# A hybrid attention and RWKV-7 layer on one core: every engine's queue in the order of the text

## The chip, the cores and the metric

The kernel runs on one NeuronCore of a Trainium2 chip. Its engines are TensorE (PE, and PEld for its weight loads), VectorE (DVE), ScalarE (ACT), GpSimd (POOL) and SyncE (SP, which here only issues transfers). Each engine works through its own queue in order; an instruction that waits for a semaphore holds all that stand behind it in that queue. The metric is the device time of one execution in microseconds, lower is better.

## The reference

One layer, float32, 256 context tokens and 1,024 latent tokens. One input projection feeds two branches whose outputs share one output projection:

```python
q, k, v, g_a, u_b, g_b = jnp.split(h @ lp['w_in'], ...)
# branch A, 8 heads, blocks of 128 queries, latents see 512 cached + 1024 own keys
s = jnp.einsum('bqhmd,bkhmd->bhmqk', qblk, k).astype(F32) * scale
p = jax.nn.softmax(s, axis=-1)
a = p[:, :, 0] - lam * p[:, :, 1]
o = jnp.einsum('bhqk,bkhv->bqhv', a, v)          # then an RMS norm over 128 values
# branch B, 16 heads of 64, both directions, one step per token
sa = jnp.einsum('bhvk,bhk->bhv', S, -kk_t)
S = S * w_t[:, :, None, :] + sa[..., None] * b_t[:, :, None, :] + v_t[..., None] * k_t[:, :, None, :]
y = jnp.einsum('bhvk,bhk->bhv', S, r_t)
# y of both directions is added, normalized per head, gated
x = x + gate[:, None, :] * (jnp.concatenate([o_a, o_b], axis=-1) @ lp['w_out'])
```

At the end comes one RMS norm per token row.

## The kernel before

**First stage.** The input projection runs 128 columns at a time over all tokens, with the preparation of both branches beside it; it spills operands to DRAM. The change leaves it as it was.

**Recurrence stage** (`mix_phase`). The scan is done in chunks of 32 tokens. An item is four pairs of heads and one segment of 256 tokens in both directions; there are 10 items of 8 chunks, so 80 calls of `step`. A step's chain is: 32 small matmuls into `bank[0]` (L895, the corrections), copies of these into the operand tile `R` (L903, the first pair of duos by ScalarE, the second by VectorE, four copies each), matmuls into `bank[1]` (L915, the new state), VectorE multiplies by the decay into the next `R` (L926), matmuls of the outputs (L938) and a ScalarE copy of them to `ys` (L940). Both sets of copies read the same PSUM bank, and the framework lets only one engine read a bank at a time, so the second engine's copies wait for the first's. Operands of two steps (a part) lie in one of two slots, and `load_part` fetches the next part into the other.

Between the pieces of the chain, `fill` puts other work, at a fixed rate per step: items of the attention (the generator `attention`), `norm` (the scan's outputs), `output`, `project` (the output projection, 10 tiles for each of four sets of columns), and the inverses that GpSimd makes for later items. Attention takes a block of 128 queries through `scores` (matmuls into `sc`, of which there are two buffers; VectorE negates, bounds by the running minimum and writes them to `pb`, L1061; after the last chunk ScalarE takes the exponential, L1069), `weight` and `combine` (VectorE: map 1 times its factor added to map 0, L1082), `trans` (TensorE transposes, a ScalarE copy to `aT`) and `values` (matmuls into `po`).

**After the recurrence** the generators run out: the last attention blocks, the last tiles of `project`, and `final`. It takes the rows of 128 tokens one after another: load `of`, `x` and the sum so far `y`; split into `ohi` (ScalarE) and `olo` (GpSimd); 24 matmuls into both banks; VectorE adds; GpSimd multiplies by the gate; VectorE adds to `x`; square, root and scaling; store. Eight of the ten rows do all this at once; the first two do their last part at the very end.

**What sets the order.** TensorE's queue has the order of the text from this stage on; the other engines' queues are sorted by the framework's scheduler, which plays the program through with estimated durations, by

```python
ctx.enter_context(tc.manual_schedule(engines={nc.tensor.engine}))
```

and `with ahead(HPC)` lets it take the recurrence's copies and multiplies earlier. In an order by hand that has no effect.

Of the kernel before, what the change touches and what calls it, by code (L numbers as in the profile page):

```python
# [10 lines left out]
F32 = mybir.dt.float32  # L11
# [37 lines left out]
TBUF = 1  # L49
YBUF = 1  # L50
NDEL = 10
# [691 lines left out]
def mix_phase(ctx, tc, i, o, s, ident, nhalf, dram, td0, neglam, subg, lnh, heads, psm):  # L743
# [137 lines left out]
    def ahead(n):  # L881
        return tc.high_priority(offset=n) if n else nullcontext()

    def step(j, k, fill):
        m, f = j // NF, j % NF
        c = HN * f + k
        p0, sg = items[m]
        hv = lambda h: slice(64 * h, 64 * h + 64)
        for w in duos:
            L, R = slots[w, j % 2]  # L890
            for d in range(2):
                for e in range(2):
                    for h in range(2):
                        u = 64 * e + 32 * h
                        nc.tensor.matmul(bank[0][u:u + 32, P * w + 64 * d:P * w + 64 * d + 64], L[0:96, e, h, d, k, 96:128],  # L895
                                         R[0:96, k, d, e, hv(h)], start=True, stop=True, tile_position=(0, u))
        with ahead(HPC):
            for w in duos:
                R = slots[w, j % 2][1]
                for e in range(2):  # L900
                    for h in range(2):
                        u = 64 * e + 32 * h
# [14 lines left out]
        with ahead(HPC):  # L917
            for w in duos:
# [9 lines left out]
        g = c // 4  # L928
        if c % 4 == 0:
            ysb[m, g] = cp.tile([P, 4, NL, HD], F32, tag="ys", name=f"ys{m}_{g}", bufs=YBUF)  # L930
# [9 lines left out]
        nc.scalar.copy(ysb[m, g][:, c % 4], bank[0][:, 256:512].rearrange("p (x v) -> p x v", x=NL))  # L940
        if later_prep:
# [3 lines left out]
    def store_y(m, g):  # L945
        p0, sg = items[m]
        y = ysb.pop((m, g))
        for d in range(2):
            t0 = tok0(sg, d)
            for h in range(2):  # L950
                q = 64 * d + 32 * h
                dst = s["y"][p0 // NL, t0:t0 + SEG, d, h].rearrange("(c t) w v -> t c (w v)", t=CH)
                dst = (dst[:, ::-1] if d else dst)[:, 4 * g:4 * g + 4]
                nc.sync.dma_start(dst, y[q:q + 32].rearrange("t c x v -> t c (x v)"))
# [6 lines left out]
    def norm(p, g0):  # L961
# [14 lines left out]
        nc.sync.dma_start(bv, s["bv"][rows, cols].rearrange("(x p) t -> p x t", p=P))  # L976
        yield
        yield
        m = pool.tile([P, 2, 4], F32, tag="m", name=f"m{nm}", bufs=2)
        r = pool.tile([P, 8], F32, tag="r", name=f"r{nm}", bufs=2)  # L980
        nc.gpsimd.tensor_tensor(y[0], y[0], y[1], op=ALU.add)
        yield
        yield
        nc.vector.tensor_reduce(m, v4(y[0]), op=ALU.add, axis=AX.X)
        nc.vector.tensor_scalar(m, m, 1.0 / HD, None, op0=ALU.mult)
        for t in range(2):
            mean = m[:, t].rearrange("p (h x) -> p h x", x=2).unsqueeze(3).broadcast_to([P, 2, 2, HD])
            nc.gpsimd.tensor_tensor(y[1][:, t].rearrange("p (x h v) -> p h x v", x=2, v=HD), y[0][:, t].rearrange("p (h x v) -> p h x v", x=2, v=HD), mean,
                                    op=ALU.subtract)
# [54 lines left out]
    def attention():  # L1044
        blocks = [(h, qb) for h in range(heads) for qb in (FORD if h == heads - 1 else range(NT))]
        st = {}

        def scores(n, m, c):
# [14 lines left out]
            if c < nk - 1:  # L1063
                return
            w = kn * nk
            ns = 1 if nk == 1 else ES
            for k in range(ns):
                v = pm[:, w // ns * k:w // ns * (k + 1)]
                nc.scalar.activation(v, v, AF.Exp, bias=mn[:, c:c + 1], scale=-1.0, accum_out=B["l"][:, m, B["b"]:B["b"] + 1])  # L1069

        def weight(n):
            h, qb = blocks[n]
            B = st[n]
            l, b = B["l"], B["b"]
            nc.vector.reciprocal(B["cc"], l[:, 1, b:b + 1])
            nc.vector.scalar_tensor_tensor(B["cc"], B["cc"], l[:, 0, b:b + 1], neglam, op0=ALU.mult, op1=ALU.mult)
# [96 lines left out]
        for n in range(NB + 2):  # L1173
# [23 lines left out]
            cost = 0.45 if nk == 3 else 0.25  # L1197
            vp = []
            if pp is not None:
                vp = [(pp, c) for c in range(1 if len(st[pp]["ch"]) > 1 else 0, len(st[pp]["ch"]))]  # L1200

            def old_values():
                if vp:
                    values(*vp.pop(0))

            for c in range(nk):
                scores(n, 0, c)
                yield cost
                if c < nk - 1 and vp:
                    old_values()  # L1210
                    yield 0.87
            while vp:
                old_values()
                yield 0.87
            for c in range(max(nk, kp_)):
                if c < kp_:
                    trans(p, c)
                    yield 0.43
                if c < nk:
                    scores(n, 1, c)  # L1220
                    yield cost
            if new:
                weight(n)
                for c in range(nk):
                    combine(n, c)
            if kp_ > 1:
                values(p, 0)
                yield 0.87
            if new and h + 1 < heads:
# [12 lines left out]

    def load_wo(nm, sl, whi, wlo, ks, g=None):
        for k in ks:
            for n in range(2):
                c = slice(n * 512, n * 512 + 512)
                w = op.tile([P, 512], F32, tag="wst", name=f"wst{nm}_{k}_{n}", bufs=2)
                nc.sync.dma_start(w, i["w_out"][0, sl[k]:sl[k] + P, c])
                if g is not None:
                    nc.gpsimd.tensor_tensor(w, w, g[:, c], op=ALU.mult)  # L1250
                nc.scalar.copy(whi[:, k, c], w)
                nc.gpsimd.tensor_tensor(wlo[:, k, c], w, whi[:, k, c], op=ALU.subtract)
                if n:
                    yield

# [132 lines left out]

    ctx.enter_context(tc.manual_schedule(engines={nc.tensor.engine}))
    att = attention()  # L1390
# [13 lines left out]
    def at(t, f):  # L1404
        later.setdefault(t, []).append(f)
# [24 lines left out]
    for t in range(n_tick):  # L1430
# [14 lines left out]
        step(j, k, fill)  # L1445
        if c % 4 == 3:
            at(t + 1, lambda m=m, g=c // 4: store_y(m, g))
        if c < NC - 1:
# [106 lines left out]
```

## Time and profile before

| | |
|---|---|
| Median of three runs | 2617.71 us (2614.24 to 2619.5) |
| Profiled execution | 2608.0 us, span 2606.2 us |
| TensorE busy, of the span | 88%, mean granted clock 0.938 |
| VectorE, ScalarE, GpSimd busy | 59%, 46%, 45% |
| Transfers over the span | 437.55 MB, mean 168 GB/s |

A busy share is an average over stages with different limits, and matmuls are pipelined, so that a busy TensorE is not one at its peak. The clock is a share of TensorE's full 2.4 GHz.

### The profile page before, as it was taken

What the parts mean: (1) busy time and instruction counts of PE and PEld (TensorE: products, weight loads), DVE (VectorE), ACT (ScalarE), POOL (GpSimd) and SP (SyncE); (2) the same over time, 40 slices, a digit from 0 to 9 for tenths busy, and PEclk for the clock granted to TensorE, in tenths of its full rate; (3) what the DMA queues carried; (4) which work ended last, traced back from release to release, by engine and by line L of the source; (5) the groups of instructions that cost most, each with busy time, mean ns of one, the idle gap of its engine ahead of it and who ended that gap; (6) DMA issues with size and microseconds to landing.
All of it is one profiled execution on the core that took longest, in us unless ns stands there. A gap on an engine that the chain in (4) does not pass through costs nothing.

```text
span 2606.2 us, 60633 instructions
## 1 busy us (share of the span) xinstructions
PE 2295.6 (88%) x23907; PEld 1895.5 (73%) x23907; DVE 1547.9 (59%) x3210; ACT 1194.9 (46%) x2530; POOL 1172.6 (45%) x1725
## 2 busy tenths in 40 slices
PE   5999999999999999898678888877998898986786
PEld 4888888888888888787466666666776676775675
DVE  5656565546455655533467776766655565665567
ACT  3334443334333343322356665655555554553353
POOL 4234343243433442465374777587722311225264
PEclk9999999999999999998789898888899998998898
DMA  7465656566646564567978797878879779868335
GB/s 240 109 162 134 176 148 179 135 164 168 151 126 168 138 181 114 171 162 173 220 146 176 155 182 140 163 156 191 205 168 220 181 182 218 193 157 242 124 118 179
DMA packets 516732, 437.55 MB, mean 168 GB/s; under 512 B 156551, under 2 KB 460851, under 8 KB 511328
## 3 DMA queue, kind: packets, MB, share of 16 engines
q1 hardware_dynamic: 514352, 427.94, 67.0%
q0 software_dynamic: 2096, 5.75, 1.1%
q8 instruction: 188, 3.08, 0.5%
q14 instruction: 96, 0.79, 0.1%
HBM read 258.69 MB, written 163.86 MB: 162 GB/s over the span
## 4 chain that ended last, share of the span: by engine, by line
PE 47%; DMA 18%; DVE 11%; POOL 9%; SPq 5%; ACT 5%; issue 4%; POOLq 0%; DVEq 0%; ACTq 0%
PE sc L1058 3%; PE pg L451 3%; DVE pb L1082 2%; PE po L1105 2%; DMA wst<-w_out 2%; PE bank L915 2%; DVE pb L1061 2%; PE pso L1299 2%; PE pa L1090 2%; DMA acc<-acc 2%; PE pso L1301 1%; PE ptk L455 1%; PE pso L1300 1%; DMA yn<-y 1%; DVE R L926 1%
## 5 line engine op out<-in xcount | busy, mean ns | idle before, releaser
L1058 PE MATMUL sc<-ka,q 128*128 128x512 f32 (+1 forms) x832 | 315.7, 470 | 73.9 <-DVE pb L1061 64.4
L1069 ACT ACTIVATE pb<-pb,mn 128x1536 f32<-128x1536 f32 (+1 forms) x160 | 218.3, 1365 | 126.6 <-DVE pb L1061 125.4
L1061 DVE TENSOR_SCALAR_CACHE_REDUCE pb<-sc,mn 128x512 f32<-128x512 f32 x256 | 191.8, 749 | 74.6 <-PE sc L1058 64.5
L1105 PEld LDWEIGHTS po<-vk,aT 128*128 128x128 f32 x1600 | 216.2, 200 | 23.9 <-ACT ob L1111 3.3
L1105 PE MATMUL po<-vk,aT 128*128 128x128 f32 x1600 | 225.4, 286 | 4.1 <-ACT ob L1111 2.0
L1058 PEld LDWEIGHTS sc<-ka,q 128*128 128x128 f32 x832 | 143.9, 213 | 110.6 <-DVE pb L1061 84.2
L736 POOL TENSOR_TENSOR tmp<-aw,tt 128x31 f32<-128x31 f32 (+15 forms) x310 | 165.4, 534 | 121.4 <-DMA L<-kt 33.6
L481 POOL TENSOR_SCALAR ta<-ta,ka 128x256 f32<-128x256 f32 x80 | 87.1, 1089 | 291.9 <-DVE bk L479 291.8
L458 ACT COPY km<-ptk 64x256 f32<-64x256 f32 x320 | 117.6, 368 | 183.1 <-PE ptk L455 149.5
L738 POOL TENSOR_TENSOR tt<-tt,tmp 128x31 f32<-128x31 f32 (+15 forms) x310 | 182.4, 589 | 20.5
L1090 PE MATMUL pa<-ident,pb 128*128 128x128 f32 x800 | 139.3, 300 | 45.5 <-DVE pb L1082 19.7
L1082 DVE SCALAR_TENSOR_TENSOR pb<-pb,cc,pb 128x512 f32<-128x512 f32 (+1 forms) x208 | 169.8, 866 | 2.3
L1090 PEld LDWEIGHTS pa<-ident,pb 128*128 128x128 f32 x800 | 105.8, 154 | 79.9 <-issue 21.9
L452 DVE TENSOR_TENSOR km<-pg,msk 128x512 f32<-128x512 f32 x80 | 55.1, 688 | 176.2 <-PE pg L451 155.0
L808 ACT COPY L<-yb 32x384 f32<-32x384 f32 x312 | 146.6, 470 | 27.5 <-PE yb L805 23.1
L903 DVE COPY R<-bank 32x128 f32<-32x128 f32 x320 | 92.6, 289 | 103.3 <-ACT R L903 92.1
L926 DVE TENSOR_TENSOR R<-bank,wc 64x256 f32<-64x256 f32 x312 | 131.0, 420 | 37.8 <-PE bank L915 28.8
L1092 ACT COPY aT<-pa 128x512 f32<-128x512 f32 (+1 forms) x208 | 116.2, 569 | 73.0 <-PE pa L1090 69.1
L1061 DVE TENSOR_SCALAR_CACHE_REDUCE pb<-sc 128x512 f32<-128x512 f32 (+1 forms) x160 | 101.4, 636 | 51.6 <-PE sc L1058 49.4
L1299 PE MATMUL pso<-wohi,ohi 128*128 128x512 f32 x240 | 104.5, 435 | 30.7 <-ACT ohi L1282 17.3
L1283 POOL TENSOR_TENSOR olo<-of,ohi 128x512 fp32r<-128x512 f32 x30 | 39.5, 1315 | 200.5 <-ACT ohi L1282 183.6
L915 PEld LDWEIGHTS bank<-R,L 128*64 128x64 f32 x2560 | 95.9, 145 | 35.5 <-issue 12.2
(355 smaller groups left out, 6432.2 us busy)
## 6 DMA issues: line engine op xcount, KB each, us to landing
kt<-km SPq DMA_DIRECT2D x160, 256.0 KB
L<-kt SPq DMA_DIRECT2D x80, 512.0 KB
acc<-acc SPq DMA_DIRECT2D x50, 512.0 KB
ra<-ra SPq DMA_DIRECT2D x160, 128.0 KB
L<-ra SPq DMA_DIRECT2D x80, 256.0 KB
R<-vb SPq DMA_DIRECT2D x160, 64.0 KB
y<-ys SPq DMA_DIRECT2D x80, 128.0 KB
yn<-y SPq DMA_DIRECT2D x40, 256.0 KB
```

The source lines that it names most:

```text
L736: e.tensor_tensor(mv, aw[:n, t, t + 1:CH].unsqueeze(2).broadcast_to([n, w, j]), tt[:n, t:t + 1, 0:j].broadcast_to([n, w, j]), op=ALU.mult)
L738: e.tensor_tensor(tt[:n, t + 1:CH, 0:j], tt[:n, t + 1:CH, 0:j], mv, op=ALU.add)
L808: nc.scalar.copy(L[96:128, :, q // 2, q % 2, :, 0:96], pp[32 * q:32 * q + 32, 0:192 * HN].rearrange("p (e c y) -> p e c y", e=2, y=96))
L915: nc.tensor.matmul(bank[1][hv(h), o_:o_ + 64], L[:, e, h, d, k, 0:64], R[:, k, d, e, hv(h)], start=True, stop=True, tile_position=(0, 64 * h))
L926: nc.vector.tensor_tensor(dst[:, :, :, hv(h)], bank[1][hv(h), 256 * w:256 * w + 256].rearrange("p (d e v) -> p d e v", e=2, d=2), wcs[p0][ ...
L1058: nc.tensor.matmul(sc, q[:, v, m, qc], ka[:, m, 0:kn], start=(v == 0), stop=(v == 1))
L1061: nc.vector.tensor_scalar(pm[:, c * 512:c * 512 + kn], sc, -0.125, mn[:, c - 1:c] if c else None, op0=ALU.mult, op1=ALU.min, accum_out=mn[ ...
L1069: nc.scalar.activation(v, v, AF.Exp, bias=mn[:, c:c + 1], scale=-1.0, accum_out=B["l"][:, m, B["b"]:B["b"] + 1])
L1082: nc.vector.scalar_tensor_tensor(a, B["p"][1][:, v], B["cc"], a, op0=ALU.mult, op1=ALU.add)
L1090: nc.tensor.transpose(pt[:, t * P:(t + 1) * P], B["p"][0][:, 512 * c + t * P:512 * c + (t + 1) * P], ident)
L1105: nc.tensor.matmul(po, B["aT"][c][:, t * P:(t + 1) * P], vk[:, t, :], start=(c == 0 and t == 0), stop=(c == last and t == nt - 1))
L1299: nc.tensor.matmul(ps, ohi[:, k - k0, :], whi[:, k, c], start=(n == 0), stop=False)
```

## The change

- `manual_schedule` names all five engines: from the recurrence stage to the end of the kernel every queue has the order of the text. The other edits move text to suit.
- Corrections: the columns of `bank[0]` are laid out by duo, so that four copies of 32x256 (two by VectorE, which comes first, two by ScalarE) take the place of eight of 32x128.
- `attention`: an exponential is written behind the item that follows its last scores; `weight` and `combine` of a block stand among the items of the next block, one at a time, and `values` runs wholly two blocks later.
- `store_y` writes each part's outputs (two chunks, 160 transfers of half the size in place of 80), from two buffers instead of one.
- `norm`: four turns between load and use instead of two; the addition of the directions and the subtraction of the mean go from GpSimd to VectorE.
- `load_wo`: a piece of the output weights is split two loads after its own load.

```diff
-YBUF = 1
+YBUF = 2
...
-        with ahead(HPC):
-            for w in duos:
-                R = slots[w, j % 2][1]
-                for e in range(2):
-                    for h in range(2):
-                        u = 64 * e + 32 * h
-                        (nc.vector.tensor_copy if w else nc.scalar.copy)(
-                            R[96:128, k, :, e, hv(h)], bank[0][u:u + 32, P * w:P * w + P].rearrange("p (d v) -> p d v", d=2))
+            R = slots[w, j % 2][1]
+            for h in range(2):
+                u = 64 * w + 32 * h
+                (nc.scalar.copy if w else nc.vector.tensor_copy)(
+                    R[96:128, k, :, :, hv(h)], bank[0][u:u + 32, 0:256].rearrange("p (d e v) -> p d e v", d=2, e=2))
...
-        yield
-        yield
+        for _ in range(4):
+            yield
...
-        nc.gpsimd.tensor_tensor(y[0], y[0], y[1], op=ALU.add)
-        yield
-        yield
+        nc.vector.tensor_tensor(y[0], y[0], y[1], op=ALU.add)
...
-            w = kn * nk
-            ns = 1 if nk == 1 else ES
-            for k in range(ns):
-                v = pm[:, w // ns * k:w // ns * (k + 1)]
-                nc.scalar.activation(v, v, AF.Exp, bias=mn[:, c:c + 1], scale=-1.0, accum_out=B["l"][:, m, B["b"]:B["b"] + 1])
+            v = pm[:, 0:kn * nk]
+            soon.append(lambda: nc.scalar.activation(v, v, AF.Exp, bias=mn[:, c:c + 1], scale=-1.0,
+                                                     accum_out=B["l"][:, m, B["b"]:B["b"] + 1]))
...
+            def item(f, r, *a):
+                f(*a)
+                if late:
+                    late.pop(0)()
+                late.extend(soon)
+                soon.clear()
+                return r
+
+            vq = [(pp, c) for c in range(len(st[pp]["ch"]))] if pp is not None else []
+            for c in range(max(nk, len(vq))):
+                if c < nk:
+                    yield item(scores, cost, n, 0, c)
+                if c == 2 and cb:
+                    combine(p, cb.pop(0))
+                if c < len(vq):
+                    yield item(values, 0.87, *vq[c])
+                if c == 1 and cb:
+                    weight(p)
+                    combine(p, cb.pop(0))
...
             for c in range(max(nk, kp_)):
+                if c < nk:
+                    yield item(scores, cost, n, 1, c)
+                if cb:
+                    combine(p, cb.pop(0))
                 if c < kp_:
...
+                    yield item(trans, 0.43, p, c)
...
-    ctx.enter_context(tc.manual_schedule(engines={nc.tensor.engine}))
+    ctx.enter_context(tc.manual_schedule(engines={e.engine for e in (nc.tensor, nc.vector, nc.scalar, nc.gpsimd, nc.sync)}))
```

VectorE's queue in the recurrence stage, before: the scores of block 1 of a head (`mn_1`; `pb_12288` is its buffer), and between them the factor and the three combinations of block 0 (`cc_0`), which stand in one run, with the copies of the corrections behind them.

```order
L1061 TENSOR_SCALAR pb_12289,mn_0_15864<-sc_0_1_2_15960,mn_0_15864 128x512
L1061 TENSOR_SCALAR pb_12288,mn_1_15970<-sc_1_0_0_15972 128x512
L1061 TENSOR_SCALAR pb_12288,mn_1_15970<-sc_1_0_1_15985,mn_1_15970 128x512
L1075 RECIPROCAL cc_0_15865<-l_0_15862 128x1
L1076 SCALAR_TENSOR_TENSOR cc_0_15865<-cc_0_15865,l_0_15862,neglam 128x1
L1082 SCALAR_TENSOR_TENSOR pb_12287<-pb_12289,cc_0_15865,pb_12287 128x512 x3
L903 COPY R_11584<-bank_12282 32x2x64 x4
L1061 TENSOR_SCALAR pb_12288,mn_1_15970<-sc_1_0_2_16035,mn_1_15970 128x512
```

VectorE's queue at such a place, after: the scores of block 6 (`mn_6`) with the combinations of block 5 (`cc_5`).

```order
L1058 TENSOR_SCALAR pb_12287,mn_6_15196<-sc_6_0_0_15198 128x512
L1058 TENSOR_SCALAR pb_12287,mn_6_15196<-sc_6_0_1_15209,mn_6_15196 128x512
L901 COPY R_11564<-bank_12282 32x4x64 x2
L1070 RECIPROCAL cc_5_15029<-l_4_14790 128x1
L1071 SCALAR_TENSOR_TENSOR cc_5_15029<-cc_5_15029,l_4_14790,neglam 128x1
L1077 SCALAR_TENSOR_TENSOR pb_12288<-pb_12289,cc_5_15029,pb_12288 128x512
L1058 TENSOR_SCALAR pb_12287,mn_6_15196<-sc_6_0_2_15262,mn_6_15196 128x512
L1077 SCALAR_TENSOR_TENSOR pb_12288<-pb_12289,cc_5_15029,pb_12288 128x512
L1058 TENSOR_SCALAR pb_12289,mn_6_15196<-sc_6_1_0_15274 128x512
L1077 SCALAR_TENSOR_TENSOR pb_12288<-pb_12289,cc_5_15029,pb_12288 128x512
```

The combinations now stand one between two scores, half a block after the exponential they need, and the copies (two, of twice the width) stand where the text has the step.

SyncE's queue near the end, before: the names carry the row of 128 tokens (`of_5_2` is row 5), `y_sample` is the store of a finished row.

```order
L1338 DMA of_3_2_27908<-oT 128x128
L1340 DMA of_3_2_27908<-oT 128x2x128
L1338 DMA of_4_2_28000<-oT 128x128
L1340 DMA of_4_2_28000<-oT 128x2x128
L1381 DMA y_sample<-y_0_2_27632 128x1024
L1344 DMA x_2_2_27809<-x_sample 128x1024
L1346 DMA y_3_2_27907<-acc 128x1024
L1338 DMA of_5_2_28100<-oT 128x128
L1340 DMA of_5_2_28100<-oT 128x2x128
L1381 DMA y_sample<-y_1_2_27718 128x1024
L1344 DMA x_3_2_27911<-x_sample 128x1024
```

SyncE's queue near the end, after.

```order
L1390 DMA y_sample<-y_2_2_27638 128x1024
L1347 DMA of_3_2_27734<-oT 128x128
L1349 DMA of_3_2_27734<-oT 128x2x128
L1353 DMA x_3_2_27737<-x_sample 128x1024
L1355 DMA y_3_2_27733<-acc 128x1024
L1130 DMA ga_7_27783<-ga 128x256
L1390 DMA y_sample<-y_3_2_27733 128x1024
L1347 DMA of_4_2_27827<-oT 128x128
L1349 DMA of_4_2_27827<-oT 128x2x128
L1353 DMA x_4_2_27830<-x_sample 128x1024
```

Before, the loads of `of` for rows 3, 4 and 5 stand ahead of the stores of rows 0 and 1. After, all loads of a row stand behind the store of the row ahead of it.

## Rows read from the trace of the kernel before

**Rows 1.** Busy time by stretch of the program (columns in its first line).

```profile
core 0: us, PE busy (x) PEld busy (x) DVE busy (x) ACT busy (x) POOL busy (x), PEclk, DMA share, GB/s
...
1236.00:2349.00 1113.00, 930.42 (x13677) 753.41 (x13676) 720.35 (x1825) 639.88 (x1460) 549.91 (x974) 0.89 0.83 180
2349.00:2516.00 167.00, 124.92 (x629) 98.86 (x628) 90.06 (x197) 58.45 (x122) 78.44 (x115) 0.88 0.57 175
2516.00:2583.00 67.00, 61.31 (x300) 48.79 (x298) 52.79 (x101) 31.36 (x66) 41.76 (x52) 1.00 0.43 144
```

**Rows 2.** TensorE's waits, recurrence stage: microseconds in total, times, longest.

```profile
PE sc L1058 <- DVE pb L1061: 61.1, 32, 8.4
...
PE bank L870 <- ACT fo L874: 7.3, 6, 3.3
...
PE bank L895 <- ACT ob L1110: 0.5, 1, 0.5
...
PE bank L870 <- DVE R L926: 0.3, 1, 0.3
```

**Rows 3.** VectorE's waits, recurrence stage.

```profile
DVE R L903 <- ACT R L903: 92.1, 45, 9.7
DVE cc L1075 <- ACT pb L1069: 40.7, 37, 4.8
DVE m L984 <- POOL yn L981: 37.2, 10, 11.0
```

**Rows 4.** ScalarE's waits, recurrence stage.

```profile
ACT pb L1069 <- DVE pb L1061: 107.3, 73, 10.6
...
ACT ohi L1282 <- DMA of<-oT: 29.8, 6, 9.4
...
ACT wohi L1251 <- DMA wst<-w_out: 28.1, 12, 6.8
```

**Rows 5.** Groups of instructions by line, recurrence stage: busy us, mean ns, idle before.

```profile
L926 DVE TENSOR_TENSOR R<-bank,wc 64x256 f32<-64x256 f32 x312 | 131.0, 420 | 37.8 <-PE bank L915 28.8 <-DMA wc<-wc 3.7
...
L903 DVE COPY R<-bank 32x128 f32<-32x128 f32 x320 | 92.6, 289 | 103.3 <-ACT R L903 92.1 <-PE yb L805 3.6
...
L981 POOL TENSOR_TENSOR yn<-yn 128x512 f32<-128x512 f32 x14 | 18.2, 1302 | 44.4 <-DMA yn<-y 32.6 <-issue 11.8
```

**Rows 6.** SyncE's queue in order of time, early in the recurrence stage.

```profile
1305.69 11.19 SPq L1248 DMA_DIRECT2D wst<-w_out  x4
...
1320.39 3.57 SPq L1248 DMA_DIRECT2D wst<-w_out  x2
```

**Rows 7.** Timeline, the output rows near the end (start us, us, instruction).

```profile
2568.46 0.43 SPq L1340 DMA_DIRECT2D of<-oT  x1
...
2570.87 1.23 DVE L1373 TENSOR_TENSOR x<-x,y 128x1024 f32<-128x1024 f32 x1 [1.89 <-POOL y L1372]
...
2571.32 0.51 ACT L1354 CAST ohi<-of 128x384 fp32r<-128x384 f32 x1 [5.36 <-DMA of<-oT]
...
2571.91 1.06 POOL L1355 TENSOR_TENSOR olo<-of,ohi 128x384 fp32r<-128x384 f32 x1 [1.08 <-ACT ohi L1354]
2572.01 0.68 DVE L1367 TENSOR_TENSOR y<-bank,y 128x512 f32<-128x512 f32 x1
...
2573.35 2.40 POOL L1372 TENSOR_TENSOR y<-y,gateb 128x1024 f32<-128x1024 f32 x1
```

**Rows 8.** Timeline, the norm of a last row.

```profile
2598.37 1.06 ACT L1377 ACTIVATE y<-x 128x1024 f32<-128x1024 f32 x1 [2.01 <-DVE y L1379]
...
2601.03 1.28 DVE L1379 SCALAR_TENSOR_TENSOR y<-x,fss,fgb 128x1024 f32<-128x1024 f32 x1
```

**Rows 9.** TensorE's timeline: 24 matmuls of a product after a gap.

```profile
2466.59 0.80 PE L1299 MATMUL pso<-wohi,ohi 128*128 128x512 f32 x1 [4.54 <-ACT ohi L1282]
...
2471.94 0.63 PE L1301 MATMUL pso<-wohi,olo 128*128 128x512 f32 x1
...
2475.98 0.39 PE L1301 MATMUL pso<-wohi,olo 128*128 128x512 f32 x1
```

More of the change, by code (lines that the diff above doesn't have):

```diff
@@ L888, in step @@
         hv = lambda h: slice(64 * h, 64 * h + 64)
-        for w in duos:
-            L, R = slots[w, j % 2]
-            for d in range(2):
-                for e in range(2):
-                    for h in range(2):
-                        u = 64 * e + 32 * h
-                        nc.tensor.matmul(bank[0][u:u + 32, P * w + 64 * d:P * w + 64 * d + 64], L[0:96, e, h, d, k, 96:128],
-                                         R[0:96, k, d, e, hv(h)], start=True, stop=True, tile_position=(0, u))
-        with ahead(HPC):
-            for w in duos:
-                R = slots[w, j % 2][1]
-                for e in range(2):
-                    for h in range(2):
-                        u = 64 * e + 32 * h
-                        (nc.vector.tensor_copy if w else nc.scalar.copy)(
-                            R[96:128, k, :, e, hv(h)], bank[0][u:u + 32, P * w:P * w + P].rearrange("p (d v) -> p d v", d=2))
+        for d in range(2):
+            for e in range(2):
+                for w in duos:
+                    L, R = slots[w, j % 2]
+                    for h in range(2):
+                        u, o_ = 64 * w + 32 * h, 128 * d + 64 * e
+                        nc.tensor.matmul(bank[0][u:u + 32, o_:o_ + 64], L[0:96, e, h, d, k, 96:128],
+                                         R[0:96, k, d, e, hv(h)], start=True, stop=True, tile_position=(0, u))
+        for w in duos:
+            R = slots[w, j % 2][1]
+            for h in range(2):
+                u = 64 * w + 32 * h
+                (nc.scalar.copy if w else nc.vector.tensor_copy)(
+                    R[96:128, k, :, :, hv(h)], bank[0][u:u + 32, 0:256].rearrange("p (d e v) -> p d e v", d=2, e=2))
         later_prep = k == HN - 1 and j + 1 < n_part
@@ L1046, in attention @@
         st = {}
+        soon, late = [], []
         def scores(n, m, c):
@@ L1197, in attention @@
             cost = 0.45 if nk == 3 else 0.25
[L1198 to L1214, printed above, removed]
+            cb = list(range(kp_))
+            def item(f, r, *a):
[16 more added lines that the diff above has]
+                    combine(p, cb.pop(0))
+            if len(cb) == kp_ and cb:
+                weight(p)
+            while len(cb) > (1 if kp_ == 3 and nk == 3 else 0):
+                combine(p, cb.pop(0))
             for c in range(max(nk, kp_)):
+                if c < nk:
+                    yield item(scores, cost, n, 1, c)
+                if cb:
+                    combine(p, cb.pop(0))
                 if c < kp_:
[L1217 to L1228, printed above, removed]
+                    yield item(trans, 0.43, p, c)
+            if not new:
+                while late:
+                    late.pop(0)()
             if new and h + 1 < heads:
@@ L1243, in load_wo, with split @@
     def load_wo(nm, sl, whi, wlo, ks, g=None):
+        got = []
+        def split():
+            w, k, c = got.pop(0)
+            if g is not None:
+                nc.gpsimd.tensor_tensor(w, w, g[:, c], op=ALU.mult)
+            nc.scalar.copy(whi[:, k, c], w)
+            nc.gpsimd.tensor_tensor(wlo[:, k, c], w, whi[:, k, c], op=ALU.subtract)
         for k in ks:
             for n in range(2):
+                if len(got) == 2:
+                    split()
                 c = slice(n * 512, n * 512 + 512)
@@ L1248, in load_wo @@
                 nc.sync.dma_start(w, i["w_out"][0, sl[k]:sl[k] + P, c])
[L1249 to L1254, printed above, removed]
+                got.append((w, k, c))
+                yield
+        while got:
+            split()
+        yield
     def project(j):
```

16 lines of the change are left out of this document (8 added, 8 removed).

## The prediction

> **What bounds the kernel now.** I read the busy times by stretch first, then the waits of each engine within the recurrence stage, then the two ends instruction by instruction. The stretches show four different kernels [rows 1]. The first stage (1,236 us) is not touched. The recurrence stage lasts 1,113.0 us for 80 steps, 13.9 us a step; TensorE is busy for 930.4 of them, so it stands for 182.6 us, and no other engine is busier than VectorE's 720 us (65%). The transfers are the second limit: 0.83 of the stage, and 0.83 times 1,113 is 924 us of full use, about what TensorE has. The end up to 2,516 has TensorE at 75%, and in the 67.0 us of the eight rows of `final` it is at 92% and full clock: these rows overlap well.
>
> TensorE's waits say who makes it stand in the stage [rows 2]. The first and the last row of those ended by VectorE are shown, of 14 that add up to 100.9 us. By far the largest, 61.1, is the scores' matmul that finds both `sc` buffers full because VectorE has not written `pb`. The twelve rows ended by ScalarE, from 7.3 to 0.5, add up to 49.5. So this stage is bound by queues that stand behind something, VectorE's first. What that is, VectorE's own waits show [rows 3]: 92.1 us in which its copies into `R` wait for ScalarE's copies out of the same bank, 40.7 in which the factor `cc` waits for an exponential, 37.2 in which the norm waits for GpSimd's additions. These three, 170 us, are what the change takes away at VectorE.
>
> **The change, term by term.** The sum is made against the profiled execution, 2,608.0 us, which lies 9.7 below the median of the runs; at the end I carry the difference over to the median.
>
> *VectorE's holds.* The new copies come first on VectorE, the combinations stand half a block behind their exponential, and the addition of the directions is VectorE's own. All three waits lose their cause. TensorE stood 100.9 us for VectorE, so no more than that can come back; VectorE is two thirds busy, and a queue this full still makes the scores wait now and then. I give back 60, with bounds of 0 and 93 (what remains is that some step is always last).
>
> *VectorE's own work.* 320 copies of 32x128 at 289 ns are 92.6 us [rows 5]. 160 of 32x256 take their place; the nearest row with 256 columns is the multiply, 420 ns, so 67 us and 25 less. Against that stand the norm's additions and subtractions: an addition of 128x512 by the row of an equal size is 0.68 us [rows 7], two half-width subtractions some 0.5 each, for 20 norms 34 us more. About nothing in sum, so the cost of the change is not in work but in order.
>
> *ScalarE's holds.* Its exponentials wait 107.3 us for VectorE's last scores [rows 4]; written behind the next item they mostly won't. But TensorE waits for ScalarE only 49.5 us, and part of that is ScalarE's work itself. I give back 15, bounds 0 and 49.5.
>
> *The start of the output weights.* SyncE is held by four and then two loads of `wst` for 11.19 and 3.57 us [rows 6], ahead of the next operands of the recurrence. In the new order they stand later, with the splits two loads behind. That is −15, bounds 0 and −18.
>
> *New holds in the stage.* An order written by hand doesn't know when a load lands. Before, the scheduler put late users behind ready ones; still GpSimd waited 32.6 us for the loads of the norm [rows 5] and ScalarE 29.8 for `of` and 28.1 for `wst` [rows 4]. The first of these is now VectorE's (the addition moved there): behind it stand copies into `R` and the scores, so TensorE sees it. The norm now has four turns instead of two between load and use, which I take to cover half: +15, bounds 0 and 32.6. For `ohi`, where behind ScalarE's wait stand the copies of the recurrence, +10 of the 29.8. The 80 more stores of `ys` are SyncE's queue time, 80 times an issue of 0.43 us [rows 7], 34 us over 1,113; SyncE has other gaps and the loads are a part ahead, so I cost them at nothing; if the loads fall behind, they are part of the second rival.
>
> The stage in sum: −60 −15 −15 +15 +10 = −65 us, to about 1,048.
>
> *The end.* Here the new order costs, and the order itself shows why: SyncE's queue has the store of row i ahead of all loads of row i+1, and that store waits for the row's last VectorE instruction. So no row can start before the one ahead is finished. One row's period, by rows: 24 matmuls; the first twelve, after a gap of 4.54 us, took from 2466.59 to 2471.94+0.63, 6.0 us, with 0.63 us for a matmul, the second twelve at 0.39 and the higher clock 3.0, together 9.0 [rows 9]. Then VectorE's addition 0.68, GpSimd's multiplication by the gate 2.40, VectorE's addition 1.23 [rows 7], and from the square to the last multiplication, 2598.37 to 2601.03+1.28, 3.94 [rows 8]: 8.25. Then SyncE: the store and two loads at 0.43, 1.3. The load lands at 2571.32, having been issued by 2568.46+0.43: 2.43. The splits take from there to 2571.91+1.06: 1.65 [rows 7]. In sum 22.6 us. Eight rows are seven periods and a last product, 7 times 22.6 plus 9.0 = 167 us, where they took 67.0 before [rows 1]: **+100**. What stands between the rows (a few transposes of the last attention block) fits into the gaps. The work behind the last product is as before. If the clock stayed at its higher level, a product would take 6.0, a period 19.6, and the eight rows 143: +76. The bounds of this term are +76 and +115 (2 us more a row for hand-overs). The same loss of lookahead meets the loads of the output weights in the 167 us ahead of it, where 16 pieces are now split in a fixed place: +10, bounds 0 and 20.
>
> The Trainium skill, in "TensorE: Matmul & The Clock Gate", Part 1, says that TensorE's default state is the throttled one and that activity releases it. By that rule each row of the new end, standing behind a gap, begins at 1.2 GHz, which gives the +100 rather than the +76; the trace agrees, with 0.63 us for a matmul soon after the 4.54 us gap and 0.39 later [rows 9].
>
> **Sum.** −65 +100 +10 = +45: 2,608.0 + 45 = 2,653 for an execution like the profiled one, and 2,617.7 + 45 = **2,662** on the median.
>
> **Rivals.**
>
> *The stage gains more than the end loses* (the other side). If nearly all of the waits for VectorE (93) and much of those for ScalarE (30) go, and the start gives 15, the stage shortens by some 135 to 978 us, and with +100 at the end the time is 2,583. For it: 182.6 us of standing TensorE, and a granted clock of 0.89 that rises when TensorE stands less. Against it: the transfers' 924 us would be 0.94 of 978, while they are at 0.83 now. It decides from a stage of about 1,000 us: below, the kernel is faster.
>
> *The text's order holds more than it frees.* If VectorE stands for its loads for the full 32.6, ScalarE for the full 29.8, and ScalarE's second place in the corrections' bank becomes the recurrence's own wait (its two copies now follow VectorE's 0.84 us, which over 80 steps is at most 67, partly paid back by the shorter copies), the stage keeps its 1,113 us and the whole end is lost: +110 to +130, about 2,735. For it: an order by hand has no lookahead, as at the end. Against it: the waits that are removed are the three largest of VectorE.
>
> *A cheaper end.* With the higher clock throughout (+76) and no loss ahead of it, −65 + 76 gives 2,629.
>
> **How the numbers follow.** The end's mechanism is nearly certain from the order; its size is known to 20 us; the stage is open between −135 and +20. Chances: the forecast 0.46, the first rival 0.27, the second 0.17, the cheap end 0.10. 0.2% is about 5 us, what a measurement of this kernel can tell from no change. Faster holds the first rival and a little of the cheap end, 0.29; the same 0.05; slower 0.66. The range takes the first rival's 2,583 in, and the second's 2,735 with 10 us for its unknowns: 2,580 to 2,745; the forecast's own range is 2,625 to 2,700.
>
> **What would show it.** Right: in VectorE's waits no `R` for ScalarE and no `cc` for the exponential; TensorE's wait for `pb` well under 61.1; a recurrence stage near 1,048 us; in the end each row's store, loads, splits and product one after another, 20 to 23 us a row, with TensorE standing between and its clock below 1.00. Wrong: a stage under 1,000 us; rows of the end that overlap; a large new wait of VectorE or ScalarE for a load in the stage.

## The result

The changed kernel takes 2,915.47 us (median of four runs, 2,904.27 to 2,921.86) where the kernel before took 2,618.61: a ratio of 1.1131, 95% interval 1.1094 to 1.1169. Slower was forecast, with 2,662 us and a range that ended at 2,745, so the size was missed by far more than the range allowed. The profiled execution has a span of 2,912.8 us against 2,606.2: 306.6 us to explain.

Busy time by stretch of the changed kernel; the columns and the three stretches (recurrence stage, end, eight rows of `final`) answer to [rows 1]:

```profile
core 0: us, PE busy (x) PEld busy (x) DVE busy (x) ACT busy (x) POOL busy (x), PEclk, DMA share, GB/s
1236.00:2472.00 1236.00, 937.77 (x13545) 750.34 (x13544) 703.38 (x1695) 608.50 (x1293) 520.03 (x931) 0.85 0.76 159
2472.00:2723.00 251.00, 157.18 (x807) 120.16 (x805) 106.10 (x245) 64.72 (x137) 68.27 (x107) 0.80 0.43 135
2723.00:2900.00 177.00, 83.41 (x292) 62.06 (x292) 53.91 (x112) 33.01 (x66) 38.72 (x46) 0.69 0.22 75
```

The recurrence stage is 123 us longer, not 65 shorter. The end ahead of the last rows took 167 us and takes 251, +84; the eight rows took 67 and take 177, +110; what follows is 10 us shorter. The borders of these stretches are not the same events in both kernels: 177 us holds also the last row's norm and store, which 67 does not. By events, the first multiplication by the decay comes 12.5 us later than before, from there to the last one it takes 118 us more, from there to the first matmul of the eight rows 81 more, and the eight products, first matmul to end of the last, take 161.9 us for 67.1, +95; what follows them is as before. These five are the 306.6.

TensorE's busy time in the stage is almost what it was (938 for 930). So it stands 298 us instead of 183, and for others than before. By the engine that ended the wait, all rows of its waits in the stage added up: VectorE 67.7 (before 100.9), ScalarE 77.3 (49.5), transfers 60.3 (20.6), GpSimd 87.6 (6.4).

TensorE's waits in the stage, after (total, times, longest):

```profile
PE pso L1310 <- POOL olo L1292: 67.0, 12, 21.4
PE yb L805 <- DMA Tb<-td: 60.3, 14, 10.0
PE sc L1055 <- DVE pb L1058: 29.2, 23, 7.1
```

The same two of its waits, for `Tb` and for `olo`, before:

```profile
PE yb L805 <- DMA Tb<-td: 11.7, 3, 7.0
...
PE pso L1301 <- POOL olo L1283: 1.4, 1, 1.4
```

What the forecast looked at came true: the scores' wait for VectorE fell from 61.1 to 29.2 [rows 2]. But the waits for the low part `olo` of an output row and for the inverses' load `Tb`, 13.1 us together before, are 127.3: they grew by over three times what that gave.

VectorE's, ScalarE's and GpSimd's waits in the stage:

```profile
DVE yn L979 <- DMA yn<-y: 11.5, 4, 6.5
...
DVE cc L1070 <- ACT pb L1063: 2.0, 3, 1.0
...
ACT R L901 <- DVE R L901: 91.5, 37, 27.4
...
ACT wohi L1249 <- DMA wst<-w_out: 57.1, 11, 16.9
ACT pb L1063 <- DVE pb L1058: 54.6, 33, 9.3
ACT ohi L1291 <- DMA of<-oT: 51.0, 11, 11.4
...
POOL tt L731 <- DMA td<-tt: 57.1, 8, 9.8
```

In the groups by line, the one of GpSimd's first and last multiplication of an inverse (both have 31 columns, so two of each of nine inverses), with its idle time behind the bar, after and then before:

```profile
L736 POOL TENSOR_TENSOR tmp<-aw,tt 128x31 f32<-128x31 f32 x18 | 4.5, 248 | 152.6 <-DMA aw<-kt 52.0 <-DMA vk<-va 47.2 <-DMA y<-ys 45.4
```

```profile
L736 POOL TENSOR_TENSOR tmp<-aw,tt 128x31 f32<-128x31 f32 x18 | 4.7, 262 | 91.7 <-DMA L<-kt 33.6 <-DMA aw<-kt 30.5 <-DMA oT<-ga 21.0
```

Against [rows 3]: the factor's 40.7 is 2.0, and VectorE waits no more for ScalarE's copies; ScalarE now waits 91.5 for VectorE's, 92.1 the other way round. GpSimd stands 152.6 us ahead of these instructions. The row names three transfers because it goes by the last event seen; by the timelines it is the inverse's own load: each of the nine inverses begins 2.4 to 5.2 us after the last of its sixteen loads is issued. One of them, on SyncE, GpSimd, ScalarE and TensorE, from 1,904 to 1,928 us:

```profile
1915.62 7.18 SPq L728 DMA_DIRECT2D aw<-kt  x16
...
1925.76 0.23 POOL L736 TENSOR_TENSOR tmp<-aw,tt 128x31 f32<-128x31 f32 x1 [31.32 <-DMA aw<-kt]
1926.07 0.27 POOL L738 TENSOR_TENSOR tt<-tt,tmp 128x31 f32<-128x31 f32 x1
1926.29 1.26 POOL L1292 TENSOR_TENSOR olo<-of,ohi 128x512 fp32r<-128x512 f32 x1
...
1904.11 0.60 ACT L1291 CAST ohi<-of 128x512 fp32r<-128x512 f32 x1
...
1905.85 0.40 PE L1309 MATMUL pso<-wolo,ohi 128*128 128x512 f32 x1
1927.60 0.79 PE L1310 MATMUL pso<-wohi,olo 128*128 128x512 f32 x1 [21.36 <-POOL olo L1292]
```

The 16 loads of `aw` are issued by 1,922.8. The text has their first user one turn behind them, so GpSimd has nothing else ahead of it and stands 31.32 us. `olo` stands two places behind, ready since ScalarE wrote `ohi` at 1,904.7, and TensorE stands 21.36 us for it in the middle of a product. Of the 31.32 us, 21 pass before SyncE issues the first of the 16 loads, so SyncE's own order has a part in them. SyncE itself stands for stores whose data are not there yet. Two of its rows from 1,236 to 2,447 us, for the stores of `ys` and for those at a norm's end (L1006); the one wait of 19.9 us ends at 1,894.9, ahead of the loads shown here:

```profile
SPq L952 <- ACT ys L938: 67.1, 12, 9.1
...
SPq L1006 <- DVE bv L1003: 25.0, 3, 19.9
```

The end, one row, all engines (ahead of it the store of the row before):

```profile
2745.05 0.34 SPq L1390 DMA_DIRECT2D y_sample<-y  x1
2745.49 0.37 SPq L1347 DMA_DIRECT2D of<-oT  x1
2745.90 0.79 SPq L1349 DMA_DIRECT2D of<-oT  x1
...
2750.17 0.51 ACT L1363 CAST ohi<-of 128x384 fp32r<-128x384 f32 x1 [1.66 <-DMA of<-oT]
...
2750.73 0.79 PE L1308 MATMUL bank<-wohi,ohi 128*128 128x512 f32 x1 [2.51 <-ACT ohi L1363]
...
2758.83 0.39 PE L1310 MATMUL bank<-wohi,olo 128*128 128x512 f32 x1
...
2760.03 2.35 POOL L1381 TENSOR_TENSOR y<-y,gateb 128x1024 f32<-128x1024 f32 x1 [7.86 <-DVE y L1376]
...
2762.41 1.23 DVE L1382 TENSOR_TENSOR x<-x,y 128x1024 f32<-128x1024 f32 x1 [1.80 <-POOL y L1381]
...
2763.67 1.06 ACT L1386 ACTIVATE y<-x 128x1024 f32<-128x1024 f32 x1 [6.62 <-DVE x L1382]
...
2764.84 1.28 ACT L1500 ACT_TABLE_LOAD   x1
...
2766.83 1.28 ACT L1063 ACT_TABLE_LOAD   x1
...
2767.34 1.28 DVE L1388 SCALAR_TENSOR_TENSOR y<-x,fss,fgb 128x1024 f32<-128x1024 f32 x1
...
2768.65 0.34 SPq L1390 DMA_DIRECT2D y_sample<-y  x1
```

Here the links follow one another as forecast. From the first store at 2,745.05 to the eighth at 2,897.88 are seven periods of 21.8 us in the mean; 22.6 was worked out. A product begins with matmuls of 0.63 to 0.79 us and ends with 0.39, and the granted clock of the stretch is 0.69, where it was 1.00. The Trainium skill, "TensorE: Matmul & The Clock Gate", Part 1, has the clock throttled until activity releases it; the trace agrees, row after row.

### The profile page after: what moved, and what is told of

Its sections match the earlier page's. It is cut to its first block, busy times and chain, and to the rows that moved or that the text cites. A ratio compares the mean times of both kernels' runs of the same rounds, so it can differ in the third digit from the quotient of the medians.

```text
span 2912.8 us, 60557 instructions
## 1 busy us (share of the span) xinstructions
PE 2352.2 (81%) x23907; PEld 1922.9 (66%) x23907; DVE 1537.6 (53%) x3110; ACT 1167.2 (40%) x2370; POOL 1126.6 (39%) x1665
## 5 line engine op out<-in xcount | busy, mean ns | idle before, releaser
L1063 ACT ACTIVATE pb<-pb,mn 128x1536 f32<-128x1536 f32 (+1 forms) x160 | 218.3, 1365 | 92.1 <-DVE pb L1058 79.9
L1085 PE MATMUL pa<-ident,pb 128*128 128x128 f32 x800 | 138.5, 300 | 56.2 <-DVE pb L1077 24.3
L1310 PE MATMUL pso<-wohi,olo 128*128 128x512 f32 x240 | 113.2, 472 | 87.1 <-POOL olo L1292 86.6
L1308 PE MATMUL pso<-wohi,ohi 128*128 128x512 f32 x240 | 115.3, 480 | 69.1 <-ACT ohi L1291 48.5
L1310 PEld LDWEIGHTS pso<-wohi,olo 128*128 128x128 f32 x240 | 54.5, 227 | 112.1 <-POOL olo L1292 100.0
```

Of the source, the lines that this page charges most:

```text
L1063: soon.append(lambda: nc.scalar.activation(v, v, AF.Exp, bias=mn[:, c:c + 1], scale=-1.0, accum_out=B["l"][:, m, B["b"]:B["b"] + 1]))
L1085: nc.tensor.transpose(pt[:, t * P:(t + 1) * P], B["p"][0][:, 512 * c + t * P:512 * c + (t + 1) * P], ident)
L1310: nc.tensor.matmul(ps, olo[:, k - k0, :], whi[:, k, c], start=False, stop=(n == len(ks) - 1))
```

## The experiments

A common measure serves all of them: the recurrence from the first to the last multiplication by decay (start times of that line's instructions); from there to the end of the span; and the first to the last matmul with `wohi` on a whole row in `final` (ten rows, of which the first two do only part of their work there; 76 such records in each run). All but the last column are of the profiled executions, which lie up to 11 us off the median of their kernel, so a difference of 10 us between two rows of the table says little. Ratios are to the kernel before as it ran beside each run, with medians of 2,616.75 to 2,624.36 us.

| kernel | recurrence, us | rest, us | ten rows, us | median, us |
|---|---|---|---|---|
| before | 1,095.9 | 264.7 | 90.4 | 2,618.61 |
| changed | 1,214.1 | 440.6 | 184.1 | 2,915.47 |
| text's order on TensorE alone | 1,085.9 | 278.2 | 85.4 | 2,608.05 |
| on TensorE and VectorE | 1,085.5 | 324.4 | 121.7 | 2,657.6 |
| on TensorE, VectorE, ScalarE | 1,112.2 | 380.9 | 149.9 | 2,737.39 |
| all five, in the stage only | 1,213.6 | 277.6 | 84.4 | 2,741.56 |
| kernel before with the order alone | 1,265.1 | 432.7 | 194.6 | 2,949.9 |
| changed, turns ahead of inverses | 1,171.3 | 440.9 | 183.3 | 2,874.87 |
| changed, loads ahead of products | 1,212.2 | 376.8 | 120.4 | 2,847.1 |
| both of these | 1,168.5 | 376.7 | 120.4 | 2,810.77 |
| both, and `Tb` first | 1,129.5 | 376.9 | 120.2 | 2,764.81 |
| all five, in the stage only, with these moves | 1,140.3 | 282.6 | 86.7 | 2,679.7 |
| TensorE alone, with the three moves in the stage | 1,083.1 | 272.7 | 83.9 | 2,616.41 |
| kernel before with the four copies alone | 1,094.3 | 267.5 | 93.1 | 2,614.43 |

### Which queues' order costs

The edit is one line, the set of engines:

```diff
-    ctx.enter_context(tc.manual_schedule(engines={e.engine for e in (nc.tensor, nc.vector, nc.scalar, nc.gpsimd, nc.sync)}))
+    ctx.enter_context(tc.manual_schedule(engines={nc.tensor.engine}))
```

> The changed kernel with TensorE alone in the text's order again; every other edit (four copies, late exponentials, combinations among the next block's items, half-size stores, norm on VectorE) stays, and the scheduler sorts the other four queues. Theory 1 (the loss comes from the written order of the other queues, which puts loads behind stores and splits behind waits): 2,600 to 2,640 us, the three stretches back at about 1,113, 167 and 67 us. Theory 2 (the edits of the text cost by themselves, as VectorE and ScalarE now copy one behind the other and VectorE has the norm's additions): still above 2,700 us, with the recurrence stage above 1,180.

2,608.05 us, ratio to the kernel before 0.9962 (0.9946 to 0.9979). Theory 1 holds: without the written order the whole loss is gone, and the other edits are worth a little. In the stage, TensorE's waits of this run:

```profile
PE sc L1055 <- DVE pb L1058: 35.5, 35, 5.0
PE yb L805 <- DMA Tb<-td: 22.5, 5, 13.5
PE pxo L1143 <- POOL ob L1137: 16.9, 5, 5.7
PE bank L913 <- ACT R L901: 16.8, 5, 9.0
```

Its waits for VectorE add up to 73.9 (before 100.9), but those for transfers to 33.5 (20.6), for ScalarE to 60.4 (49.5), for GpSimd to 16.9 (6.4): for the 27 us given back at VectorE, 34 came up elsewhere. Over the stretch of its own stage it is busy 917.63 us of 1,107:

```profile
1236.00:2343.00 1107.00, 917.63 (x13604) 743.17 (x13602) 715.49 (x1701) 610.73 (x1296) 520.27 (x932) 0.89 0.81 181
```

It stands 189 us, not less than the 183 before. The recurrence is 10 us shorter, no more, and even that is no larger than the scatter of single executions.

The same line in the kernel before (`+` all five engines), nothing else changed:

> The kernel before with all five engines in the text's order and nothing else changed. Theory 1: as slow as the changed kernel or slower, 2,900 to 3,050 us, since the edits of the text that suit the order are missing and the combinations again stand right behind their exponential. Theory 2: close to the kernel before, under 2,700 us.

2,949.9 us, 1.1264 (1.1239 to 1.1289), as theory 1 had it. The edits that were to suit the text's order win back 34 of 331 us.

With `engines={nc.tensor, nc.vector, nc.scalar}` and with TensorE and VectorE only (each by its `.engine`):

> The changed kernel with TensorE, VectorE and ScalarE in the text's order, SyncE and GpSimd sorted by the scheduler. Theory 1a (the queues that hold are SyncE's, with loads behind stores, and GpSimd's, with the recurrence's inverses behind the splits): the recurrence stage returns to about 1,080 to 1,130 us and the whole to 2,620 to 2,700; the last rows take 12 to 16 us each instead of 21.8, because a split on ScalarE still stands behind the square of the row ahead. Theory 1b (VectorE's and ScalarE's written order holds by itself): the stage stays above 1,190 us and the whole above 2,800.

> The changed kernel with TensorE and VectorE in the text's order, the scheduler sorting ScalarE, SyncE and GpSimd. If VectorE's written order is harmless, as the prediction had it: 2,600 to 2,640 us. If it costs by itself, as much as SyncE's and GpSimd's: 2,680 to 2,740, with the last rows at 10 us or more each.

2,737.39 (1.0426 to 1.0490) and 2,657.6 (1.0104 to 1.0153). Neither theory had it whole, and the second time lies between its two ranges: the recurrence of the first returned, as 1a said, to 1,112.2, 16 above the kernel before, but the total is over 1a's 2,700, since ScalarE's and VectorE's order cost in the end. Added in this sequence, VectorE's order costs the recurrence nothing (1,085.5 for 1,085.9) and the rest 46 us; ScalarE's adds 27 and 57; SyncE's and GpSimd's the other 102 and 60. ScalarE's order without VectorE's, and SyncE's without GpSimd's, were not run. In the end, VectorE's own waits of the run with TensorE and VectorE, and ScalarE's of the run with three engines:

```profile
DVE acc L1302 <- DMA acc<-acc: 34.4, 5, 13.6
...
DVE x L1382 <- POOL y L1381: 30.7, 10, 6.2
```

```profile
ACT y L1386 <- DVE x L1382: 76.4, 8, 13.2
```

The addition to `x` waits for GpSimd's multiplication by the gate, the square for that addition, and the next row's split stands behind the square. So the chain of SyncE's store and loads is not the only one that puts the rows in a line: the eight products, 67.1 us before, 68.8 with TensorE alone in the text's order and 161.9 in the changed kernel, take 94.3 us with VectorE's order added and 125.9 with ScalarE's, while SyncE is still sorted.

> The changed kernel with the text's order on all five engines in the recurrence stage only; from its end on TensorE alone is in that order. Both theories of the stage leave it at about 1,236 us here. If the loss after the stage (440 us instead of 257 from its end) is the written order's, it goes: 2,720 to 2,750 us. If part of it is work that the slower stage leaves over, more than 2,780.

The edit closes the order by hand where the recurrence ends and opens one for TensorE alone:

```diff
+        hand.close()
+        ctx.enter_context(tc.manual_schedule(engines={nc.tensor.engine}))
         cp_.close()
```

2,741.56 us (1.0448 to 1.0505). The rest returns to 277.6, what it is with TensorE alone in the text's order (278.2), so the loss behind the stage, but for the 13 us between these and the kernel before, is the written order's own, and 1,213.6 in the recurrence stays.

### What in the stage, what in the end

Ten more turns between the loads of an inverse and their use:

```diff
-    yield
+    for _ in range(1 + INVL):
+        yield
...
-            while state["ninv"] < 33 * (state["t"] + INVA + _ / 4 + pos / 2) / NC:
+            while state["ninv"] < (33 + INVL) * (state["t"] + INVA + _ / 4 + pos / 2) / NC:
```

> The changed kernel, all five queues in the text's order, with ten more turns between the sixteen loads of the operands of an inverse and GpSimd's first instruction on them (and a rate that keeps the inverse's end where it was). Theory 1 (in the recurrence stage GpSimd stands for these loads, and TensorE behind it for the inverses and for the split part olo): GpSimd's waits for these loads and for the store of the inverse ahead, about 200 us now, fall below 60, TensorE's 127 us for Tb and olo below 50, the stage shortens by 70 to 110 us and the whole to 2,800 to 2,850. Rival (GpSimd stands because ScalarE's and VectorE's written order brings it its inputs late): the stage stays within 30 us, the whole above 2,880.

2,874.87 us (1.0927 to 1.0995), 41 less than the changed kernel, and by the profiled executions 43 less in the recurrence: less than the 70 expected, but the rival's 2,880 isn't reached either. Its rows say why:

```profile
PE yb L807 <- DMA Tb<-td: 58.9, 17, 8.2
...
PE pso L1312 <- POOL olo L1294: 21.3, 12, 5.1
...
POOL tt L733 <- DMA td<-tt: 17.1, 3, 8.6
```

```profile
L738 POOL TENSOR_TENSOR tmp<-aw,tt 128x31 f32<-128x31 f32 x18 | 4.4, 245 | 66.3 <-DMA y<-ys 41.0 <-DMA vk<-va 14.9 <-DMA oT<-ga 9.6
```

GpSimd's idle time at the inverses' loads fell from 152.6 to 66.3 and TensorE's wait for `olo` from 67.0 to 21.3: that was GpSimd standing for these loads. With its wait for the store of the inverse ahead GpSimd still stands 83 us, not under 60. The wait for `Tb` stayed (58.9 for 60.3): I had put it down to late inverses, wrongly.

The other half, the loads of the next row behind this row's splits, for `project` and for `final`:

```diff
             nc.gpsimd.tensor_tensor(olo[:, 0:KS], of[:, 0:KS], ohi[:, 0:KS], op=ALU.subtract)
+            if n_t + 1 < len(TORD) and ready(TORD[n_t + 1]):
+                nxt = load_of(TORD[n_t + 1])
...
+            if n_r + 1 < len(seq) and ready(*seq[n_r + 1]):
+                nxt = front(*seq[n_r + 1])
             for n in range(2):
                 half(row, n)
                 yield
+            if nxt is not None:
+                split(nxt)
+            post(row)
```

> The changed kernel, all five queues in the text's order, with the text written so that the loads of the next row of the output projection stand right behind the splits of this one (ahead of its product and store) and, in the last rows, the next row's splits ahead of this row's gate and norm. Theory (rows in a line are all of the loss at the end): the last eight rows take 75 to 95 us instead of 177, the stretch ahead of them loses 40 to 80 of its 84 us, the recurrence stage stays at 1,200 to 1,240; 2,730 to 2,790 in all. Rival (only the first link, loads behind the store, matters little beside the chain of ScalarE and VectorE): more than 2,850.

2,847.1 us (1.0824 to 1.0893): outside the expected 2,730 to 2,790, and under the rival's 2,850 by little. The ten rows fell from 184.1 to 120.4 and the eight products from 161.9 to 106.8, not to 75 to 95, and the stretch ahead of them lost nothing (64 of the rest's 64 us are the rows'). TensorE's two largest waits in that stretch, in the changed kernel (2,472 to 2,730 us) and then in this run (2,470 to 2,700 us):

```profile
PE pso L1308 <- ACT ohi L1291: 35.6, 8, 11.3
PE pso L1310 <- POOL olo L1292: 19.6, 6, 7.0
```

```profile
PE pso L1320 <- POOL olo L1300: 26.5, 5, 9.7
PE pso L1318 <- ACT ohi L1299: 25.5, 6, 8.8
```

Before, the two were 14.7 and 1.2 us. So there TensorE stands for the splits on ScalarE and GpSimd, 55 us and still 52 with the loads ahead; what holds the splits was not taken apart.

> The edits of the two runs ahead of it together: ten more turns in front of an inverse, and loads ahead of products and stores. If the two losses add up, the whole is 2,620 to 2,690 us; if the rest of the stage's loss is VectorE's and ScalarE's order, it stays above 2,700.

2,810.77 us (1.0681 to 1.0748). The two edits add up (−41 and −68 against −105 together), and the total is still above 2,700, so they are not all.

For the wait for `Tb`, on top of both edits, one move and one more:

```diff
+        load_inv(j)
         for w in duos:
             p = p0 + 2 * w
             L, R = slots[w, j % 2]
...
-            at(t + 1, lambda m=m, g=c // HN: store_y(m, g))
+            at(t + 2, lambda m=m, g=c // HN: store_y(m, g))
```

> The run with ten more turns before an inverse and loads ahead of products, and in addition the next part's load of the inverse (Tb) issued first among the part's loads and the stores of ys one step later, behind these loads. If TensorE's remaining wait for Tb (67 us) comes from SyncE, whose queue has four stores that wait for ScalarE and two loads ahead of it: the wait falls below 25 us, the recurrence stage from 1,187 to about 1,140, the whole to 2,750 to 2,785. If the single buffer of Tb sets the time of its load: no change, above 2,795.

2,764.81 us (1.0513 to 1.0582), 46 less, 39 of them in the recurrence; the rival's single buffer is not it. TensorE's rows at this place hold no `Tb` (67.3 us in the run ahead of it); instead it waits 29.6 us for another load of the part, where there was no such wait:

```profile
PE yb L807 <- DMA L<-kt: 29.6, 10, 5.6
```

Whether the order of the loads or the later stores did it was not tried apart.

> The text's order on all five engines in the recurrence stage only, with the three moves and the loads of the projection's rows ahead; the scheduler sorts the end. If the stage with these moves is near 1,140 us and the end as in the kernel before: 2,640 to 2,680. If the end has work left over from the stage: above 2,700. Under 2,610 would say that a written order with loads ahead beats the scheduler's.

2,679.7 us (1.0177 to 1.0230), at the upper end of what was expected: recurrence 1,140.3, rest 282.6. A written order with loads ahead still loses to the scheduler's.

### The edits that are worth keeping

Only the corrections' layout and the four copies, in the kernel before:

> The kernel before, its scheduler untouched, with only the corrections laid out by duo and emptied in four copies of 32x256. If the copies' serial turns at the bank were on the path: 2,590 to 2,610 us, VectorE's wait for ScalarE at this place from 92 us to under 40. If that wait was only where VectorE stood anyway: 2,612 to 2,625.

2,614.43 us against 2,621.53 beside it, 0.9975 (0.9956 to 0.9995): about a quarter of one per cent, close to what can be told. VectorE's wait for ScalarE at this place is gone; ScalarE waits 56.2 for VectorE. The time fits the second expectation: the wait of 92 us was for the most part where VectorE stood anyway. The copies themselves in this run:

```profile
L901 DVE COPY R<-bank 32x256 f32<-32x256 f32 x160 | 67.0, 419 | 62.6 <-PE bank L895 52.5 <-ACT acc L1289 4.2 <-ACT ob L1109 2.5
...
L901 ACT COPY R<-bank 32x256 f32<-32x256 f32 x158 | 57.6, 364 | 61.6 <-DVE R L901 56.2 <-PE po L1103 2.7
```

> TensorE alone in the text's order, every other edit of the change, and the same three moves in the text (ten more turns before an inverse, Tb first, stores of ys a step later). The scheduler places loads itself, so the moves should matter little: 2,595 to 2,612 us, as the run with TensorE alone. If the scheduler is led by where the text has the loads: under 2,590.

2,616.41 against 2,624.36 beside it, 0.9969 (0.9950 to 0.9988): as without the three moves (0.9962). The 2,595 to 2,612 us were missed by 4, as the kernel before, too, ran slower beside this run than beside the other (2,624.36 for 2,616.75). The scheduler doesn't need the moves. The run with TensorE alone in the text's order is the version that beats both kernels, the one before by 0.4%.

## Why the prediction was wrong

Slower was right, but in the profiled execution +45 us were forecast and +307 found. Nearly all of the miss lies in two places: the stage (−65 forecast, 131 us more measured, 12.5 of them ahead of the first multiplication by the decay) and the stretch ahead of the last rows (+10 forecast, +81 measured). The last rows were right.

- **The last rows: +100 forecast, +95 measured.** 21.8 us a row for 22.6; the clock fell. Single links are off and cancel: from the square to the last multiplication 4.95 us in the row shown for 3.94 (a table load lies between), the load 3.5 for 2.43, from the first split to the first matmul 0.6 for 1.65, the product 8.5 for 9.0. The store ahead of the loads was taken for the only thing that puts the rows in a line; VectorE's and ScalarE's order, without it, already give 59 of the 95 us.
- **The output weights and the stretch ahead of the last rows: +10 forecast, +81 measured.** I saw that stores stand ahead of loads in `final` and did not look for the same order in `project`, whose tiles read their row behind the store of the one ahead. But loads ahead did not mend it. TensorE's waits for the splits there, 16 us before and 55 after, are about half of the loss; what holds the splits is open, beyond that it is the written order (277.6 for the rest without it) and that VectorE and ScalarE have a share.
- **New holds in the stage: +25 forecast, the step that failed most.** I priced the norm's loads at VectorE and `of` at ScalarE, from the rows where these engines waited before. VectorE's hold for `yn` turned out at 11.5 us, and VectorE's order as a whole cost the stage nothing; ScalarE's waits for `of` and `wst` grew from 57.9 to 108.1 us. I left GpSimd's queue out: it carries nine inverses, each behind 16 loads, and the splits `olo` that TensorE needs in mid-product. The kernel before has the same wait, 91.7 us of idle time at this group in its own profile; there TensorE waits only 6.4 us for GpSimd, and 87.6 after. I had not read that row: a wait that costs nothing under a scheduler can cost under a written order.
- **The stores of `ys` and SyncE's queue: cost at nothing, the second failure.** A queue is an order, not a sum: `Tb` stood behind stores that wait for ScalarE. TensorE's wait for it went from 11.7 to 60.3 us; the two moves brought 39 us of the recurrence back. The second rival, with no gain in the stage, came nearer, and ScalarE's second place in the corrections' bank did become a wait (91.5 us); but it named ScalarE and VectorE as what would hold and had neither SyncE's place nor GpSimd's.
- **VectorE's holds: −60 forecast, at most −10 found.** The waits went, as predicted, and so did TensorE's for VectorE in part (33 us). But with the scheduler on the other queues the stage gained only 10 us; TensorE's standing did not shrink but moved to transfers, ScalarE and GpSimd. The step "what TensorE stood for VectorE can come back" fails: where many waits of a few microseconds lie close together, the next one takes the place of the one removed. That is how I read these rows; no run isolates it.
- **ScalarE's holds and the start of the output weights: −15 each forecast, no gain found.** The exponentials' wait for VectorE fell, from 107.3 to 54.6 us, but TensorE's waits for ScalarE rose from 49.5 to 77.3. The loads of `wst` did leave the start of the stage, but the third load of a part there is issued at 1,340.8 us, behind the inverses' loads and the stores of `ys`, where it was 1,324.0.
- **Work: right.** VectorE's copies took 419 ns (420 taken), the norm's addition 702 and its subtraction 440 (680 and 500).

In sum, over the stage: −33 us of waits for VectorE, +28 for ScalarE, +40 for transfers, +81 for GpSimd, and 7 more of work make the +123. By the experiments the loss of 128 us in the recurrence against the run with TensorE alone is 43 for GpSimd at the inverses' loads (which SyncE issues late, so that both queues are in it), 39 for SyncE's order at `Tb` and `ys`, 3 for the loads of output rows, and 44 that stay; ScalarE's written order, which cost 27 with SyncE and GpSimd sorted, is the likely larger part of these, but they were not taken apart.

## What to carry to other kernels

Before a queue is written by hand, list for every engine, the idle ones first, the instructions that wait for a load, and what stands behind each: their waits under the scheduler, however harmless, become waits of whoever stands behind. A text that says load, use, store one after another is fine for a scheduler and is no order for a queue; lookahead must be put into it for every load, not only where the busiest engine is. And a wait at the engine that is waited for most is worth less than its row says while several others are only a few microseconds behind it.

## What was not expected of the hardware

In the row of the end shown above ScalarE loads a table twice, 1.28 us each time, once ahead of the root and once ahead of the next exponential, the first of them on the row's own chain, between the square and the last multiplication. In the stage of the changed kernel the sixteen small loads for one inverse take 7.2 to 12.0 us of SyncE's queue, and GpSimd stands up to 35.2 us for them, most of it, in the longest cases, before the first is issued.
